# A hybrid decoder layer on one core: convolution work spread out, page numbers and embedding loaded ahead, padded rows, and norm statistics by block transposes

## The chip, the cores and the metric

The kernel runs on one core of one Trainium2 chip. The metric is the time of one execution in microseconds (us); the lower, the better. The core has a matrix engine (TensorE, PE in the profile; PEld is its loading of weights), VectorE (DVE), ScalarE (ACT), GpSimd (POOL) and SyncE (SP), which here issues nearly all transfers between device memory and the on-chip buffer SBUF. Each engine takes its instructions in the order in which they were written. An instruction that has to wait holds everything behind it on its engine.

## The reference

One layer for a prompt of 2048 tokens and for 8 sequences of 4 new tokens each with 8192 cached ones, all in fp32:

```
z = rms_norm(x) @ w_in                      # q, k, v (512 each), a, gt
u = a * sigmoid(gt)
# differential attention, 4 heads: two softmax maps (ALiBi), w = p0 - lam * p1
y_attn = rms_norm(w @ v) * (1 - lam_init)
c = causal_depthwise_conv(u, width 31) + b_dw
y_conv = silu(layer_norm(c))                # 512 channels
m = concat(y_attn, y_conv) @ w_out
h = x + rms_norm(m)
f = square(relu(rms_norm(h) @ w_ff1)) @ w_ff2          # 1024 -> 4096 -> 1024
h = h + rms_norm(f)
h = h + sigmoid(h @ w_ple_gate) * (p @ w_ple)          # p: a 256-wide embedding per token
```

For the sampled tokens keys and values come from a paged cache, whose pages a table of integers names. The outputs are h for all tokens, the keys and values, and the last 30 rows of u.

## The kernel before

Tokens lie along the free axis and channels along the 128 partitions. Every large product keeps fp32 accuracy by splitting each operand into a high and a low part: `mm3` (L234 to L236) issues hi·hi, lo·hi and hi·lo, three matmuls for each 128-deep slice. `WStream` loads the weights on SyncE (L112), makes the high part on ScalarE (L121, `wide` or `wh`) and the low part on VectorE (L122, `wlo` or `wl`), a block ahead of use. A block is 24 matmuls, eight slices of one 128-row output tile.

Three stages follow one another.

*Input projection* (to about 522 us): 80 blocks of 128x512 matmuls (`zp`) over four column blocks of the prompt. Beside them, in the background queue `bgq`, VectorE does the causal convolution of the edge columns, one filter tap of one channel tile at a time (`taps`, L246; 31 taps for each of four tiles). At the second block of the last round the kernel empties that queue at once (`while bgq: bg(1)`), then puts the layer norm over channels (`convln`) for the first 416 tokens into the queue `slow`.

*Attention* (to about 1018 us): scores `scp`, transposes, products with V; besides it runs the decode stream, `decode`, for the cached tokens (until late in the third stage). It reads the page numbers from SBUF into registers on SyncE (`feed`). At its start it loads the first row of page numbers (L921), and VectorE packs two of them into one integer (L927). GpSimd issues the 32 stores of the normed attention output (`ya`, L1130).

*Dense part* (to the end): five groups of 416 tokens (`TG`). Steps of a group g: E (output projection, 8 blocks), F1 and F2 (the two MLP products, in four chunks c of 8 blocks each, two blocks of the next F1 ahead of each F2), L (embedding product, 2 half blocks) and G (gate, 8 blocks). After each block `tick` advances every generator in the list `side` by its own rate: `norm_a` and `norm_f` (the norms around the MLP), `load_y` (the next group's input from device memory) and `convln` of the next group, whose rate is `CONV[0]` and which with `gated` also does the convolution itself, two taps to a step. `settle()` runs the whole list to its end on the spot. It is called at F1 block (3, 7) of the groups 0 to 2, after which `load_y` starts, and ahead of each E. `embed` at F2 block (3, 2) loads two tiles of p (`x`, from `pT`) and at once writes their split on ScalarE (L1647) and GpSimd.

A norm's statistic in the dense part goes over the partitions: squares are added elementwise into `acc` (128x416); `Rstd.mean` multiplies `acc`, in four pieces as the stationary operand, with a column of ones (`pm`, L149; each is two records in the profile), so that the sums lie as 128x4; `seed` finds the inverse root by three Newton steps on VectorE; `spread` (L189, `rsb`) lays the result out over all partitions by four transposes on TensorE. `convln` and the second norm of `norm_a` then copy it to SBUF on ScalarE (L312, L1545).

SBUF tiles of moving rows (`bh`, `bl`, `ah`, `al`, and views of `kv`) are 416 floats wide, 1664 bytes.

Of the kernel before, what the change touches and what calls it, by code (L numbers as in the profile page):

```python
# [20 lines left out]
NB = 8  # L21
# [9 lines left out]
TG = 416  # L31
NG = 5
# [15 lines left out]
CONV = (1.45, -2.0)  # L48
# [143 lines left out]

@with_exitstack
def kernel(
# [29 lines left out]
    odec = cp.tile([128, NH, NDEC], F32, name="odec")  # L224
    ident = cc[:, C_ID:C_ID + 128]
# [11 lines left out]

    def taps(c, u, o, n, j):

        for tap in range(NTAP):  # L240
            w = col(V_DW + j * NTAP + tap)
            x = u[:, o + tap:o + tap + n]
            if tap == 0:
                V.tensor_scalar(out=c, in0=x, scalar1=w, scalar2=col(V_BDW + j), op0=ALU.mult, op1=ALU.add)
            else:
                V.scalar_tensor_tensor(out=c, in0=x, scalar=w, in1=c, op0=ALU.mult, op1=ALU.add)  # L246
            yield

    def convln(pool, bank, n0, n, tags, gated=False):
# [55 lines left out]
        r = Rstd(nc, pool, bank, ident, n)  # L305
        r.mean(acc, ones_c[:, 0:1])
        r.seed(V)
        yield
        yield
        rsb = r.spread()  # L310
        rs = cfull[:, 4, :n]
        S.activation(out=rs, in_=rsb, func=AF.Copy)  # L312
# [70 lines left out]
    with tc.manual_schedule():  # L383
# [9 lines left out]
        with (  # L393
# [155 lines left out]
            load_x(1, 6)  # L549

# [134 lines left out]

            stores = []
# [100 lines left out]
            def lambdas():  # L787
                lt = p1.tile([128, 512], F32, tag="th", name="lt", bufs=1)[:, :256]
# [23 lines left out]
            for si, (ps, it, bl) in enumerate(steps):  # L812
# [46 lines left out]
                if ps == 0:  # L859
                    if ii == 1:  # L860
                        lambdas()
                        nc.sync.dma_start(out=udec[:, :, :, 0:30], in_=st)
                    if ii in (2, 6):
                        xtile(2 + (ii == 6))
                        for k in (0, 2, 4, 6):
                            load_x(2 + (ii == 6), k)
                    if ii in (3, 7):
                        slow.append(sumsq(2 + (ii == 7)))
                    if ii == 10:
                        bgq.append(conv_dec())  # L870
                    if ii == len(items) - 1:
                        tick(100)
                        slow.append(conversion(3))
                elif ii == 1:
                    while bgq:
                        bg(1)
                    conv_stores()
                    slow.append(convln(p1, st_bank, 0, TG, P1_TAGS))
                elif ii == 10:
                    nc.sync.dma_start(out=shared, in_=tabP)  # L880
                    load_k(0, 0)
                    for n in range(3):
                        load_q(n)
# [34 lines left out]
        def load_ids(b):  # L918
            if b < NB:
                ids[b] = dc.tile([1, NPG], I32, tag="ids", name="ids")  # L920
                nc.sync.dma_start(out=ids[b], in_=pt[:, b * NPG:b * NPG + NPG])  # L921

        def pack_ids(b):
            if b < NB:
                n = ids[b][:, :].rearrange("o (n t) -> o t n", t=2)
                ids[b] = dc.tile([1, NPG // 2], I32, tag="id2", name="id2", bufs=2)
                V.scalar_tensor_tensor(out=ids[b], in0=n[:, 1, :], scalar=1024.0, in1=n[:, 0, :], op0=ALU.mult, op1=ALU.add)  # L927
# [257 lines left out]
        with tc.tile_pool(name="p2", bufs=1, reuse_waits="tile") as p2, tc.tile_pool(name="p2ps", bufs=1, space=PSUM, reuse_waits="tile") as pp:  # L1185
# [64 lines left out]
            def combine(r):  # L1250
# [4 lines left out]
                cf = p2.tile([128, 2], F32, tag="cf", name="cf", bufs=2)  # L1255
# [75 lines left out]
            for tag, w, bufs in (("m", 8, 3), ("lp", 8, 3), ("l", 8, 4), ("cf", 2, 2)):  # L1331
# [82 lines left out]
        with (  # L1414
# [22 lines left out]

            def pair():
                return small("bh", 10, F32R), small("bl", 10, F32R)
# [11 lines left out]
            def rstd(st_, wait=1):  # L1451
                r = Rstd(nc, p3, st_bank, ident, TG)
                r.mean(st_["acc"], ones_d)
                r.seed(V)
                for _ in range(wait):
                    yield
                st_["rs"] = r.spread()
# [3 lines left out]
            def in_ring():  # L1461
# [3 lines left out]
                for i in range(RING):  # L1465
                    t = ring[:, 4 * i:4 * i + 4, :].rearrange("p a b -> p (a b)")[:, :4 * TG]
                    out.append(t.rearrange("p (l k t) -> p l k t", l=2, k=2))
                return out

            def load_y(g):  # L1470
                if g + 1 < NG:
                    yh = p3.tile([128, 8, TG], F32R, tag="ah", name="yh")
                    yl = p3.tile([128, 8, TG], F32R, tag="al", name="yl")
# [24 lines left out]
            def norm_a(g, fast):  # L1498
# [5 lines left out]
                def load(k):  # L1504
                    xs_[k] = small("bh", 10) if fast else small("x", 2)
# [6 lines left out]
                xh = p3.tile([128, 8, TG], F32R, tag="ah", name="xh")  # L1512
                xl = p3.tile([128, 8, TG], F32R, tag="al", name="xl")
# [24 lines left out]
                yield from rstd(nxt)  # L1538
                st_["rs2"] = small("rs")
                S.activation(out=st_["rs2"], in_=nxt["rs"][:, :TG], func=AF.Copy)  # L1540
# [100 lines left out]
            def embed(g):  # L1641
                h2s[g, "p"] = []
                for k in range(2):
                    p_ = small("x", 2)
                    nc.sync.dma_start(out=p_, in_=pT[:, k, g * TG:g * TG + TG])
                    ah, al = pair()
# [61 lines left out]

            def settle():
# [6 lines left out]
            pair()  # L1716
            small("acc", 2)
            small("rs")
            p3.tile([128, 8, TG], F32R, tag="al", name="yl")
            big(0)  # L1720
            big(1)
            for i in ("sq", "r", "x"):
                small(i, 2)
            for _ in load_y(0):
# [3 lines left out]
            for s_ in steps:  # L1728
                kind, g = s_[0], s_[1]
                first = s_[2:] in ((0,), (0, 0))  # L1730
                if kind == "F1" and first:
# [8 lines left out]
                    if g + 1 < NG:  # L1740
# [4 lines left out]
                            convln(p3, st_bank, (g + 1) * TG, TG, tags, not last), 1.0 if last else CONV[0], -4.0 if last else CONV[1],  # L1745
# [145 lines left out]
```

## Time and profile before

| | |
|---|---|
| time, median of 3 runs | 3175.6 us (3173.62 to 3176.58) |
| the profiled execution | 3175.43 us |
| its span, first to last instruction | 3173.6 us |
| mean granted clock of TensorE | 0.984 |
| TensorE matmul records | 18992 |
| transfers | 649.44 MB, 205 GB/s on average |

The page and the views of the trace come from that one profiled execution. A line such as `PE mm L234 <- ACT wide L121` reads: a TensorE instruction of line 234 that writes `mm` stood idle until ScalarE's instruction of line 121 had written `wide`. In timelines a row gives start, length, engine, line, operation, output and inputs with shapes, and in brackets the idle time ahead with what ended it. Line numbers are those of the kernel before.

### The profile page before, as it was taken

The numbers are of one execution on the slowest core, as the hardware profiler recorded it, in microseconds if no ns is written. First come the engines' busy times: TensorE is split into PE (matmuls) and PEld (weight loads), VectorE is DVE, ScalarE is ACT, GpSimd is POOL, SyncE is SP. The second block draws the span as 40 slices with busy tenths as digits, with TensorE's granted clock in tenths as the row PEclk, the third lists the DMA queues.
The fourth block names the chain that finished last, engine by engine and source line by source line (L and its number), as shares of the span: only waits on it lengthen the run. The fifth ranks groups of instructions, "written<-read, shape, count | busy, mean of one in ns | idle before, by whom it ended". The sixth has DMA issues, their size and how long they took to land.

```text
span 3173.6 us, 54936 instructions
## 1 busy us (share of the span) xinstructions
PE 3046.8 (96%) x18992; PEld 2680.0 (84%) x18992; DVE 2039.8 (64%) x3601; ACT 1240.9 (39%) x2248; POOL 978.6 (31%) x1063
## 2 busy tenths in 40 slices
PE   8999897999999899989999989999989999999999
PEld 6877686867778688878888878888889999999998
DVE  7889663887885677645768536767557453664444
ACT  4333223776775322224322235322244333432233
POOL 2552213766774310122301124200134121320023
PEclk9999898999999999999999989999999999999999
DMA  5445367988897876786976777877544344433334
GB/s 179 131 131 111 105 174 218 306 263 272 275 290 256 292 258 224 239 286 207 310 246 223 247 276 240 303 235 237 188 167 150 121 141 162 127 109 119 114 118 135
DMA packets 316520, 649.44 MB, mean 205 GB/s; under 512 B 45872, under 2 KB 98864, under 8 KB 315984
## 3 DMA queue, kind: packets, MB, share of 16 engines
q1 hardware_dynamic: 313680, 637.53, 62.4%
q0 software_dynamic: 2560, 8.39, 0.7%
q8 instruction: 150, 2.46, 0.3%
q14 instruction: 130, 1.06, 0.1%
HBM read 581.60 MB, written 64.18 MB: 203 GB/s over the span
## 4 chain that ended last, share of the span: by engine, by line
PE 80%; DVE 7%; DMA 3%; ACT 3%; issue 2%; POOL 2%; SPq 1%; POOLq 0%; DVEq 0%; ACTq 0%
PE mm L234 19%; PE mm L235 18%; PE mm L236 18%; PE zp L234 4%; PE zp L235 4%; PE zp L236 4%; PE dacc L1067 3%; PE ds L994 3%; PE scp L1219 3%; PE tp L1283 1%; DVE acd L653 1%; DVE wlo L122 1%; ACT S L1241 1%; DMA x<-pT 1%; PE pm L149 1%
## 5 line engine op out<-in xcount | busy, mean ns | idle before, releaser
L122 DVE TENSOR_TENSOR wlo<-wide 128x1024 fp32r<-128x1024 f32 x410 | 523.6, 1278 | 668.3 <-PE mm L235 236.1
L234 PE MATMUL mm<-bh,wide 128*128 128x416 f32 x1616 | 582.9, 361 | 25.0 <-ACT wide L121 23.9
L121 ACT ACTIVATE wide<-wide 128x1024 fp32r<-128x1024 f32 x410 | 430.8, 1053 | 411.0 <-DMA wide<-ff 252.5
L235 PE MATMUL mm<-bh,wlo 128*128 128x416 f32 x1616 | 573.7, 355 | 6.9 <-DVE wlo L122 6.8
L236 PE MATMUL mm<-bl,wide 128*128 128x416 f32 x1616 | 574.3, 355 | 0.0
L358 POOL TENSOR_TENSOR r<-r 128x416 f32<-128x416 f32 x160 | 156.4, 979 | 1067.2 <-ACT bh L1577 1067.1
L234 PE MATMUL mm<-xh,wide 128*128 128x416 f32 x1280 | 455.8, 356 | 0.0
L236 PE MATMUL mm<-xl,wide 128*128 128x416 f32 x1280 | 450.9, 352 | 0.9 <-DVE xl L1530 0.9
L235 PE MATMUL mm<-xh,wlo 128*128 128x416 f32 x1280 | 448.5, 350 | 1.5 <-DVE wlo L122 1.5
L234 PEld LDWEIGHTS mm<-bh,wide 128*128 128x128 f32 x1616 | 307.4, 190 | 56.2 <-ACT wide L121 29.1
L235 PEld LDWEIGHTS mm<-bh,wlo 128*128 128x128 f32 x1616 | 308.3, 191 | 15.6 <-DVE wlo L122 11.0
L236 PEld LDWEIGHTS mm<-bl,wide 128*128 128x128 f32 x1616 | 307.4, 190 | 4.6
L1577 ACT ACTIVATE bh<-r 128x416 fp32r<-128x416 f32 x160 | 88.2, 552 | 484.0 <-DVE r L1576 484.0
L246 DVE SCALAR_TENSOR_TENSOR ct<-ct,vc 128x416 f32<-128x416 f32 x360 | 270.6, 752 | 8.4
L234 PE MATMUL zp<-xh,wh 128*128 128x512 f32 x640 | 258.9, 404 | 10.0 <-ACT wh L121 8.5
L234 PEld LDWEIGHTS mm<-xh,wide 128*128 128x128 f32 x1280 | 240.6, 188 | 28.2 <-issue 19.6
L235 PE MATMUL zp<-xh,wl 128*128 128x512 f32 x640 | 253.3, 396 | 8.1 <-DVE wl L122 8.1
L236 PE MATMUL zp<-xl,wh 128*128 128x512 f32 x640 | 253.6, 396 | 3.6 <-DVE xl L530 3.6
L235 PEld LDWEIGHTS mm<-xh,wlo 128*128 128x128 f32 x1280 | 241.1, 188 | 5.5 <-DVE wlo L122 2.4
L236 PEld LDWEIGHTS mm<-xl,wide 128*128 128x128 f32 x1280 | 240.5, 188 | 3.6 <-DVE xl L1530 1.2
L1241 ACT ACTIVATE S<-S,m 128x512 f32<-128x512 f32 (+3 forms) x320 | 207.0, 649 | 47.3 <-DVE m L1224 46.3
L246 DVE SCALAR_TENSOR_TENSOR cv<-u,vc,cv 128x416 f32<-128x416 f32 (+1 forms) x240 | 202.9, 845 | 6.9
(249 smaller groups left out, 5119.9 us busy)
## 6 DMA issues: line engine op xcount, KB each, us to landing
wide<-ff SPq DMA_DIRECT2D x320, 512.0 KB, 4.2
kv<-ck SPq DMA_DIRECT2D x512, 256.0 KB, 4.3
kv<-cv SPq DMA_DIRECT2D x512, 256.0 KB, 4.0
wr<-w_in SPq DMA_DIRECT2D x40, 512.0 KB, 4.0
wide<-w_out SPq DMA_DIRECT2D x40, 512.0 KB, 3.3
wide<-gate SPq DMA_DIRECT2D x40, 512.0 KB, 3.8
wide<-qs SPq DMA_DIRECT2D x64, 256.0 KB, 6.3
ya<-ct SPq DMA_DIRECT2D x40, 208.0 KB, 2.1
```

The costliest lines, as they stand in the source:

```text
L121: self.nc.scalar.activation(out=hi, in_=r, func=AF.Copy)
L122: self.lo_eng(self.ns).tensor_tensor(out=lo, in0=r, in1=hi.bitcast(F32), op=ALU.subtract)
L234: T.matmul(out, wh, xh, start=start, stop=False)
L235: T.matmul(out, wl, xh, start=False, stop=False)
L236: T.matmul(out, wh, xl, start=False, stop=stop)
L246: V.scalar_tensor_tensor(out=c, in0=x, scalar=w, in1=c, op0=ALU.mult, op1=ALU.add)
L358: P.tensor_tensor(out=out, in0=a, in1=b, op=ALU.mult)
L994: T.matmul(ps[32 * k:32 * k + 32, o:o + 128 * n], qz[:, b % 2, h, :], ring[:, g:g + 4 * n, h * 128 + 32 * k:h * 128 + 32 * k + 32], start= ...
L1067: T.matmul(acc[32 * s:32 * s + 32, :], wts[u // 2 * 2][:, u % 2, 32 * s:32 * s + 32], t[i][:, s, :], start=(u == 0), stop=(s > 0 and u == ...
L1219: T.matmul(ps[:, :wp], q[:, c, l, r % 2 * 128:r % 2 * 128 + 128], kt[:, n0 % 1024:n0 % 1024 + wp], start=(l == 0), stop=(l == 1),)
L1241: S.activation(out=st_[c][:, o:e], in_=st_[c][:, o:e], func=AF.Exp, scale=-1.0, bias=st_["m"][:, c, last:last + 1], accum_out=st_["lp"][:, ...
L1577: S.activation(out=ah, in_=r, func=AF.Square)
```

## The change

Seven edits, all on order, layout and the dense part's norms; the arithmetic of matmuls stays.

1. In the projection the background queue isn't emptied at the second block: `after_conv` lets `convln` start only when the convolutions have left the queue at their usual pace, four taps a block.
2. The first row of page numbers is loaded behind the first tiles of x and packed in `lambdas` into `idp0`, a tile that lives through the kernel; `load_ids` and `pack_ids` skip row 0.
3. In the dense part `settle()` at F1 (3, 7) is gone; `behind` starts `load_y` when the entry ahead of it in `side` has ended. `CONV[0]` rises from 1.45 to 1.62.
4. `embed` is split: `load_p` at F2 (3, 0), `embed` at F2 (3, 3); for the last group at G 0 and G 3 (before G 2).
5. The 15 norms of the MLP and the four gated `convln` use `Turned`: VectorE transposes `acc` in 32x32 blocks, sums over each block's 32 columns to 128x13, one product with the block matrix `C_G` adds over partitions, Newton as before, and VectorE's block transpose of the broadcast result lays it out. ScalarE's copies go.
6. Moving rows get a pitch of `TP` = 448 floats, 1792 bytes; tile `cf` grows from 2 to 24 floats.
7. The scratch for GpSimd's transfer descriptors is 8192 bytes instead of 16384.

```diff
+TP = 448
-CONV = (1.45, -2.0)
+CONV = (1.62, -2.0)
+class Turned:
+    def gather(self, acc, turned):
+        V = self.nc.vector
+        self.part = self.small("rsp", 1)
+        V.transpose(turned, acc)
+        V.tensor_reduce(out=self.part, in_=turned.rearrange("p (b f) -> p b f", f=32), axis=AX.X, op=ALU.add)
+    def mean(self):
+        self.pm = self.bank("pm")
+        self.nc.tensor.matmul(self.pm[:, :self.nb], self.same, self.part, start=True, stop=True)
+    def seed(self, scale):
...
+    def spread(self, out):
+        self.nc.vector.transpose(
+            out.rearrange("p (b f) -> p b f", f=32),
+            self.y.rearrange("p (b o) -> p b o", o=1).to_broadcast([128, self.nb, 32]),
+        )
+        return out
...
+    idp0 = cp.tile([1, NPG // 2], I32, name="idp0")
...
+        if turned:
+            r = Turned(nc, pool, bank, cc[:, C_G:C_G + 128], n)
+            r.gather(acc, tl("sq"))
+            yield
+            yield
+            r.mean()
+            r.seed(1.0 / 512)
+            yield
+            r.spread(rs)
...
+            ids0 = p1.tile([1, NPG], I32, name="ids0")
+            nc.sync.dma_start(out=ids0, in_=pt[:, 0:NPG])
...
+            def after_conv(it, convs):
+                while any(c in bgq for c in convs):
+                    yield
+                while cstores:
+                    conv_stores()
+                yield from it
...
-                    while bgq:
-                        bg(1)
-                    conv_stores()
-                    slow.append(convln(p1, st_bank, 0, TG, P1_TAGS))
+                    slow.append(after_conv(convln(p1, st_bank, 0, TG, P1_TAGS), list(bgq)))
...
+            def moving(tag, dt=F32R):
+                return p3.tile([128, TP], dt, tag=tag, name=tag, bufs=10)[:, :TG]
...
+            def eight(tag, name):
+                return p3.tile([128, 8, TP], F32R, tag=tag, name=name)[:, :, :TG]
...
-            def rstd(st_, wait=1):
-                r = Rstd(nc, p3, st_bank, ident, TG)
-                r.mean(st_["acc"], ones_d)
-                r.seed(V)
-                for _ in range(wait):
-                    yield
-                st_["rs"] = r.spread()
+            def rstd(st_, out=None):
+                r = Turned(nc, p3, st_bank, cc[:, C_G:C_G + 128], TG)
+                r.gather(st_["acc"], small("sq", 2))
+                yield
+                r.mean()
+                r.seed(1.0 / 1024)
+                st_["rs"] = r.spread(st_bank("rsb")[:, :TG] if out is None else out[:, :])
...
+            def behind(e, it):
+                while e in side:
+                    yield
+                yield from it
...
                 if kind == "F1" and s_[2:] == (3, 7):
                     evacuate(0)
                     if g + 2 < NG:
-                        settle()
-                        side.append([load_y(g + 1), 1.0, 0.0])
-                if kind == "F2" and s_[2:] == (3, 2) and g != NG - 2:
+                        side.append([behind(side[-1] if side else None, load_y(g + 1)), 1.0, 0.0])
+                if kind == "F2" and s_[2:] == (3, 0) and g != NG - 2:
+                    load_p(min(g, NG - 2))
+                if kind == "F2" and s_[2:] == (3, 3) and g != NG - 2:
                     embed(min(g, NG - 2))
-                if s_ == ("G", NG - 2, 2):
+                if s_ == ("G", NG - 2, 0):
+                    load_p(NG - 1)
+                if s_ == ("G", NG - 2, 3):
                     embed(NG - 1)
...
-    nc = _bacc.Bacc("TRN2", target_bir_lowering=False, num_devices=1)
+    nc = _bacc.Bacc("TRN2", target_bir_lowering=False, num_devices=1, dynamic_dma_scratch_size=8192)
```

Where instructions move is seen in the order on an engine. VectorE in the input projection, at the second block of the last round, before: `cv` is the convolution, `wl` the weights' low part, `u` the convolution's input, `cmean` the channel mean that TensorE makes.

```order
L122 TENSOR_TENSOR wl<-wr,wh 128x1024
L653 SCALAR_TENSOR_TENSOR acd<-udec,vc,acd 128x32 x19
L244 TENSOR_SCALAR cv<-u,vc 128x384
L246 SCALAR_TENSOR_TENSOR cv<-u,vc,cv 128x384 x30
L122 TENSOR_TENSOR wl<-wr,wh 128x1024 x3
L775 SCALAR_TENSOR_TENSOR u<-th,fa 128x512
L293 TENSOR_TENSOR ct<-ct,cmean 128x416 x4
```

The same place in the changed kernel:

```order
L123 TENSOR_TENSOR wl<-wr,wh 128x1024
L717 SCALAR_TENSOR_TENSOR acd<-udec,vc,acd 128x32 x19
L297 TENSOR_SCALAR cv<-u,vc 128x384
L299 SCALAR_TENSOR_TENSOR cv<-u,vc,cv 128x384 x3
L123 TENSOR_TENSOR wl<-wr,wh 128x1024
L299 SCALAR_TENSOR_TENSOR cv<-u,vc,cv 128x384 x8
L123 TENSOR_TENSOR wl<-wr,wh 128x1024
L299 SCALAR_TENSOR_TENSOR cv<-u,vc,cv 128x384 x4
```

The 30 taps in one piece are now pieces of 3 to 8 between weight splits, and the mean's subtraction comes later.

ScalarE in the dense part where group 0 calls `settle`, before: L319 and L327 are the last steps of `convln`, `bh<-r` evacuates F1, `bh<-x` is `embed`.

```order
L319 ACTIVATE sq<-ct,hlb 128x416
L121 ACTIVATE wide<-wide 128x1024
L1577 ACTIVATE bh<-r 128x416 x2
L319 ACTIVATE sq<-ct,hlb 128x416
L327 ACTIVATE ct<-ct 128x416
L319 ACTIVATE sq<-ct,hlb 128x416
L327 ACTIVATE ct<-ct 128x416
L319 ACTIVATE sq<-ct,hlb 128x416
L327 ACTIVATE ct<-ct 128x416 x2
L121 ACTIVATE wide<-wide 128x1024 x2
```

The same steps in the changed kernel, where they begin earlier:

```order
L381 ACTIVATE sq<-ct,hlb 128x416 x2
L1156 ACTIVATE sc<-dacc 128x512
L122 ACTIVATE wide<-wide 128x1024
L389 ACTIVATE ct<-ct 128x416
L122 ACTIVATE wide<-wide 128x1024
L1654 ACTIVATE bh<-r 128x416
L381 ACTIVATE sq<-ct,hlb 128x416
L389 ACTIVATE ct<-ct 128x416
L122 ACTIVATE wide<-wide 128x1024
```

Seven of the norm's steps stood between two weight splits; now one or two do.

VectorE at the start of attention, before: L1224 takes a row of scores with its maximum, L1256 to L1258 are softmax's sums, L927 packs page numbers.

```order
L1224 ISA m 128x1
L1256 TENSOR_REDUCE l<-lp 128x2
L1257 RECIPROCAL cf<-l 128x1
L1258 SCALAR_TENSOR_TENSOR cf<-l,nlam,cf 128x1
L927 SCALAR_TENSOR_TENSOR id_4369<-ids 1x32
L1256 TENSOR_REDUCE l<-lp 128x2
L1257 RECIPROCAL cf<-l 128x1
L1258 SCALAR_TENSOR_TENSOR cf<-l,nlam,cf 128x1
L1224 ISA S_4388,m<-scp,shared 128x512
```

In the changed kernel:

```order
L1330 SCALAR_TENSOR_TENSOR cf<-l,nlam,cf 128x1
L1328 TENSOR_REDUCE l<-lp 128x2
L1329 RECIPROCAL cf<-l 128x1
L1330 SCALAR_TENSOR_TENSOR cf<-l,nlam,cf 128x1
L1296 ISA S_4330,m<-scp,shared 128x384
L1296 ISA m 128x1
L1296 ISA S_4337,m<-scp,shared 128x384
L1296 ISA m 128x1
L1296 ISA S_4342,m<-scp,shared 128x512
```

The row L927 is gone there (its like stands in the projection), so a row of scores follows the sums of the row before it directly.

More of the change, by code (lines that the diff above doesn't have):

```diff
@@ L190, in spread, with __init__, small @@
         return r[:, :self.n]
+class Turned:
+    def __init__(self, nc, pool, bank, same, n):
+        self.nc, self.pool, self.bank, self.same, self.n, self.nb = nc, pool, bank, same, n, n // 32
+    def small(self, tag, bufs=2):
+        return self.pool.tile([128, 16], F32, tag=tag, name=tag, bufs=bufs)[:, :self.nb]
+    def gather(self, acc, turned):
[7 more added lines that the diff above has]
+    def seed(self, scale):
+        V = self.nc.vector
+        x, y, t = self.small("rsx", 1), self.small("rsy"), self.small("rst", 1)
+        V.tensor_scalar(out=x, in0=self.pm[:, :self.nb], scalar1=scale, scalar2=EPS, op0=ALU.mult, op1=ALU.add)
+        V.tensor_scalar(
+            out=y.bitcast(I32), in0=x.bitcast(I32), scalar1=-0.5, scalar2=1597463007.0, op0=ALU.mult, op1=ALU.add
+        )
+        for _ in range(3):
+            V.tensor_tensor(out=t, in0=y, in1=x, op=ALU.mult)
+            V.scalar_tensor_tensor(out=t, in0=t, scalar=-0.5, in1=y, op0=ALU.mult, op1=ALU.mult)
+            V.scalar_tensor_tensor(out=y, in0=t, scalar=1.5, in1=y, op0=ALU.add, op1=ALU.mult)
+        self.y = y
+    def spread(self, out):
+        self.nc.vector.transpose(
+            out.rearrange("p (b f) -> p b f", f=32),
+            self.y.rearrange("p (b o) -> p b o", o=1).to_broadcast([128, self.nb, 32]),
+        )
+        return out
 @with_exitstack
@@ L236, in mm3, with pack @@
         T.matmul(out, wh, xl, start=False, stop=stop)
+    def pack(out, ids):
+        n = ids[:, :].rearrange("o (n t) -> o t n", t=2)
+        V.scalar_tensor_tensor(out=out, in0=n[:, 1, :], scalar=1024.0, in1=n[:, 0, :], op0=ALU.mult, op1=ALU.add)
     def taps(c, u, o, n, j):
@@ L304, in convln @@
         yield
-        r = Rstd(nc, pool, bank, ident, n)
-        r.mean(acc, ones_c[:, 0:1])
-        r.seed(V)
-        yield
-        yield
-        rsb = r.spread()
-        rs = cfull[:, 4, :n]
-        S.activation(out=rs, in_=rsb, func=AF.Copy)
+        rs = cfull[:, 4, :n]
+        if turned:
[7 more added lines that the diff above has]
+            r.spread(rs)
+        else:
+            r = Rstd(nc, pool, bank, ident, n)
+            r.mean(acc, ones_c[:, 0:1])
+            r.seed(V)
+            yield
+            yield
+            S.activation(out=rs, in_=r.spread(), func=AF.Copy)
         yield
@@ L923, in pack_ids @@
         def pack_ids(b):
[L924 to L925 removed]
+            if 0 < b < NB:
+                raw = ids[b]
                 ids[b] = dc.tile([1, NPG // 2], I32, tag="id2", name="id2", bufs=2)
[L927 removed]
+                pack(ids[b], raw)
+        ids[0] = idp0
         def decode():
@@ L1511, in norm_a @@
                 yield from rstd(st_)
-                xh = p3.tile([128, 8, TG], F32R, tag="ah", name="xh")
-                xl = p3.tile([128, 8, TG], F32R, tag="al", name="xl")
+                xh, xl = eight("ah", "xh"), eight("al", "xl")
                 xs2[g] = [(xh[:, k, :], xl[:, k, :]) for k in range(8)]
@@ L1537, in norm_a @@
                     yield
-                yield from rstd(nxt)
-                st_["rs2"] = small("rs")
-                S.activation(out=st_["rs2"], in_=nxt["rs"][:, :TG], func=AF.Copy)
+                rs2 = small("rs")
+                yield from rstd(nxt, rs2)
+                st_["rs2"] = rs2
                 yield
@@ L1645, in embed @@
                     nc.sync.dma_start(out=p_, in_=pT[:, k, g * TG:g * TG + TG])
+                    h2s[g, "x"].append(p_)
+            def embed(g):
+                h2s[g, "p"] = []
+                for p_ in h2s[g, "x"]:
                     ah, al = pair()
@@ L1716 @@
             pair()
+            eight("al", "yl")
             small("acc", 2)
-            small("rs")
-            p3.tile([128, 8, TG], F32R, tag="al", name="yl")
             big(0)
@@ L1723 @@
                 small(i, 2)
+            eight("ah", "yh")
             for _ in load_y(0):
```

30 lines of the change are left out of this document (15 added, 15 removed).

## Prediction

> **What bounds the kernel now.** I read the page's totals first, then the list of what TensorE waits for, then busy times stretch by stretch around its longest stops.
>
> ```profile
> span 3173.6 us, 54936 instructions
> PE 3046.8 (96%) x18992; PEld 2680.0 (84%) x18992; DVE 2039.8 (64%) x3601; ACT 1240.9 (39%) x2248; POOL 978.6 (31%) x1063
> ```
>
> TensorE works 3046.8 of 3173.6 us. The profiled execution took 3175.4 us (its span and 1.8 around it), 0.2 under the median of the runs, 3175.6; I sum against 3175.4 and read the result as a median. About 127 us are not TensorE work, so a change can win only these, or make TensorE's own work shorter. The waits, as total, times, longest:
>
> ```profile
> PE mm L234 <- ACT wide L121: 23.9, 6, 7.0
> PE mm L235 <- DVE wlo L122: 10.4, 16, 1.0
> PE cmean L290 <- POOL shared L355: 5.8, 1, 5.8
> ```
>
> Few and long waits: the places matter, not the averages. The next view gives such places, with three undisturbed stretches for comparison. Its columns: stretch, length, busy time (and count) of PE, PEld, DVE, ACT and POOL, TensorE's granted clock (PEclk), DMA share, GB/s.
>
> ```profile
> 325.00:360.00 35.00, 21.55 (x74) 16.40 (x73) 16.63 (x25) 4.43 (x7) 5.38 (x4) 0.76 0.49 157
> 515.00:560.00 45.00, 28.94 (x130) 22.16 (x128) 22.68 (x84) 21.04 (x59) 19.18 (x30) 0.81 0.86 240
> 600.00:1000.00 400.00, 379.74 (x3666) 299.48 (x3665) 320.29 (x922) 278.98 (x735) 281.76 (x391) 1.00 0.87 273
> 1100.00:1370.00 270.00, 269.07 (x1728) 236.47 (x1727) 186.02 (x283) 74.83 (x101) 39.69 (x41) 1.00 0.72 241
> 1250.00:1300.00 50.00, 50.00 (x286) 42.72 (x286) 42.56 (x58) 13.53 (x17) 11.19 (x10) 1.00 0.80 270
> 1370.00:1390.00 20.00, 14.23 (x61) 13.27 (x60) 9.55 (x11) 6.47 (x10) 6.92 (x7) 0.83 0.64 207
> 1395.00:1410.00 15.00, 11.51 (x68) 9.94 (x70) 4.79 (x6) 5.48 (x8) 6.27 (x5) 0.89 0.84 296
> 1840.00:1860.00 20.00, 14.49 (x80) 12.30 (x80) 10.32 (x13) 6.46 (x10) 7.23 (x8) 0.74 0.58 200
> 1868.00:1885.00 17.00, 12.53 (x75) 10.54 (x74) 6.01 (x8) 5.54 (x9) 6.26 (x5) 0.80 0.81 295
> 2305.00:2340.00 35.00, 26.55 (x126) 24.97 (x125) 17.73 (x29) 13.26 (x21) 13.12 (x13) 0.85 0.57 199
> 3050.00:3115.00 65.00, 62.46 (x330) 60.10 (x329) 37.69 (x51) 29.71 (x47) 27.43 (x22) 1.00 0.35 113
> ```
>
> Length less PE busy is idle time. A stop also costs clock: the granted clock falls to half two to five us into a long stop and stays there for 3.4 to 10.2 us. I count that loss as (1 − PEclk) × length, less half of the idle time that lies inside the half-clock part (found by narrowing the stretches: 7.6 us of idle in 325–360, 8.2 in 515–560, 1.0 in 1370–1390, 3.3 in 1840–1860, 1.6 in 1868–1885, 4.8 in 2305–2340). Undisturbed, 1100 to 1370 us, TensorE is idle 0.93 of 270 us while VectorE is busy 69%.
>
> **The change, part by part.** *Input projection.*
>
> ```profile
> 314.21 21.58 DVE L246 SCALAR_TENSOR_TENSOR cv<-u,vc,cv 128x384 f32<-128x384 f32 x30
> ```
>
> VectorE's timeline shows 30 filter taps done in one go, 21.6 us, and TensorE stops at 329 us for the weight split (`wl`) queued behind them. A second stop is the channel mean behind GpSimd's sums (5.8, above). 325–360: idle 13.45, clock 0.24 × 35 = 8.4 less half of 7.6 idle = 4.6. Now the taps come four to a block and the norm starts behind them; the same work lies beside matmuls. **−18.1.** If the pace left a stop, it would be one split's delay, counted in the leftovers.
>
> *Page numbers.* At the start of attention VectorE's queue, in order, holds the packing of page numbers:
>
> ```profile
> 539.56 0.18 DVE L927 SCALAR_TENSOR_TENSOR id<-ids 1x32 int32<-1x32 int32 x1 [10.54 <-DMA ids<-pt]
> ```
> ```profile
> wide<-qs SPq DMA_DIRECT2D x6, 256.0 KB, 9.2
> ```
>
> VectorE stands 10.54 us for a load (`ids<-pt`) that the load queue has behind V and K parts. Loaded in the projection, it is gone; its 0.18 us of packing stays, elsewhere. 515–560 holds 16.1 idle and 0.19 × 45 = 8.6 less half of 8.2 = 4.5 clock: 20.5. Not all returns: the attention's own query tiles of the same queue take 9.2 us to land (second row's median, in 515–560), and the next are issued just behind. Bounds −4 and −15; I take **−10**.
>
> *Settle.* Before, three of the five groups force the convolution's norm to its end at the last FF1 block. ScalarE's timeline there:
>
> ```profile
> 1371.09 0.64 ACT L319 ACTIVATE sq<-ct,hlb 128x416 f32<-128x416 f32 x1 [2.31 <-DVE ct L317]
> ...
> 1377.81 1.99 ACT L121 ACTIVATE wide<-wide 128x1024 fp32r<-128x1024 f32 x2
> ```
>
> For 6.7 us ScalarE follows VectorE through the norm's last steps, and two weight splits stand behind them: the 23.9 us row of waits. Now the norm ends by its own pace, a weight split between any two of its steps, and its eight stores lie between weight loads. Idle 5.77 + 5.51 + 7.5 (of 8.45; 0.9 is the embedding's) = 18.8; clock 0.17 × 20 less 0.5, 0.26 × 20 less 1.7, 0.15 × 35 less 2.4 = 9.0. **−27.8.** Next in time is the load of the next group's input, `yh`, which is now let go by the norm's end and needed only with the next output projection, after eight FF2 blocks of some 4.5 us (24 matmuls, 0.19 apart): the same place as before.
>
> *Embedding.* ScalarE's in-order queue holds the split of a tile whose load was issued just then:
>
> ```profile
> 1398.86 1.10 ACT L1647 ACTIVATE bh<-x 128x416 fp32r<-128x416 f32 x2 [6.65 <-DMA x<-pT]
> ```
>
> Issued three blocks of 4.5 us ahead, 13 us against the 6.65 waited, the load lands before its split. 1395–1410: 3.49 + 0.11 × 15 = 5.1. 1868–1885: 4.47 + 0.20 × 17 less 0.8 = 7.1. With 0.9 in the third group and, near the end of the program, 2.5 of 65 in the last stretch: **−15.6.**
>
> *Norms.* On TensorE one norm in the dense part reads:
>
> ```profile
> 2398.59 0.35 PE L236 MATMUL mm<-bl,wide 128*128 128x416 f32 x1
> 2398.78 0.95 PE L149 MATMUL pm<-ones_d,acc 128*128 128x1 f32 x8
> 2399.59 0.44 PE L234 MATMUL mm<-bh,wide 128*128 128x416 f32 x1
> 2399.86 0.35 PE L235 MATMUL mm<-bh,wlo 128*128 128x416 f32 x1
> ...
> 2404.22 0.60 PE L189 MATMUL rsb<-cc,rsy 128*128 128x128 f32 x4
> 2404.58 0.43 PE L234 MATMUL mm<-bh,wide 128*128 128x416 f32 x1
> ```
>
> Matmuls start 0.19 apart. The eight column records take 0.81 and the matmul behind them 0.27 instead of 0.19: 0.89. The four transposes take 0.36 and, I take it, the same 0.08: 0.44. Both go; one 128x13 product comes, between nothing and 0.44; by its two records of 0.1 and the 0.08 I take 0.2. 19 × (0.89 + 0.44 − 0.2) = **−21.5.** In exchange VectorE gets, per norm, two block transposes and a reduction:
>
> ```profile
> L1048 DVE STREAM_TRANSPOSE wt<-sc 128x256 f32<-128x256 f32 x64 | 27.5, 434 | 0.0
> L562 DVE TENSOR_REDUCE accd<-xnd 128x32 f32<-128x256 f32 x1 | 0.6, 622 | 0.0
> L246 DVE SCALAR_TENSOR_TENSOR ct<-ct,vc 128x416 f32<-128x416 f32 x360 | 270.6, 752 | 8.4
> ```
>
> By elements 2 × 0.71 + 1.01 = 2.4 us, 46 us over 19. Behind them queue the low halves of the weights (`wlo`). The convolution's pace also rises from 2.9 to 3.24 taps a block at 752 ns, at most 0.26 us more per block; its sum stays. Price for TensorE between 0 (row 1100–1370) and 46 (all of it). All `wlo` waits today are 10.4 us in 16 stops; I let them double: **+10.**
>
> *Padded rows.* Dense matmuls stream 416-column rows of 1664 bytes, 6.5 times 256, so every other one starts 128 bytes off a multiple of 256.
>
> ```profile
> 2692.64 0.35 PE L234 MATMUL mm<-kp,wide 128*128 128x416 f32 x1
> 2693.21 0.35 PE L234 MATMUL mm<-kp,wide 128*128 128x416 f32 x1
> 2693.78 0.35 PE L234 MATMUL mm<-kp,wide 128*128 128x416 f32 x1
> 2694.34 0.35 PE L234 MATMUL mm<-kp,wide 128*128 128x416 f32 x1
> ```
>
> Triples start 0.57 or 0.56 apart. Over the undisturbed ones of all 3280 the mean is 562 ns for rows on a multiple and 571 for the others. After the change rows are 1792 bytes, 7 × 256, and all have the same start; by the layout all of them, and the weights too, move to 128 past a multiple. If what counts is the row's distance to the weights, all are like today's fast half: 1640 × 9 ns = −15 (−21 if the alternation costs too). If the row's start itself counts, all are slow: +15. The trace doesn't separate them; I take the distance, since one common shift of both operands otherwise would have to matter: **−15.**
>
> The Trainium skill ("TensorE: Matmul & The Clock Gate", Part 2: What happens when you issue a matmul) says that loading weights doesn't steal SBUF read bandwidth from the running matmul, since each has a read port. By it the distance to the weights couldn't matter, and all rows would be slow, +15, a sum of 3113; this trace shows the alternation, but moves weights and rows never separately, so no row here decides.
>
> *Leftovers.* Each new product may find its sums late (`pm` waited once for `acc` before, 1.8 us), and one restart may keep part of a stop. **+6.** ScalarE's copies and the stores' new places cost nothing: ScalarE is 39% busy. The halved descriptor scratch: nothing, see the last rival.
>
> Sum: −18.1 − 10 − 27.8 − 15.6 − 21.5 + 10 − 15 + 6 = −92.0; 3175.4 − 92.0 = 3083.4, say **3083**.
>
> **Rivals.** *(a) The row's start counts.* All rows slow: 3083 + 30 = 3113. For it: only the start is known to differ between today's halves. Against: weights move as well.
> *(b) VectorE becomes the bound in the dense part.* Where the convolution is densest, 1250–1300, it is already busy 42.56 of 50. Faster taps and transposes there would hold `wlo`; if all 46 us show, 3083 + 36 = 3119. Against: 85% leaves room for 7 us per 50, and the additions are some 3.
> *(c) The attention's start does not do what is meant:* TensorE, freed at 529, stops a few us later at the next query tile, gain 0: 3093.
> *(d) Slower.* GpSimd issues attention's output stores, through descriptors in the scratch that is halved:
>
> ```profile
> q0 software_dynamic: 2560, 8.39, 0.7%
> ```
> ```profile
> DMA to landing us min/median/max: 1.9/5.4/7.8
> ```
>
> ```profile
> L1130 POOL DMA_DIRECT2D ya<-yh x16: 587/587/724, 578.8 to 1036.0; - x16
> ```
>
> 32 stores, in 16 pairs, of 80 packets each. If the descriptors of two consecutive ones no longer fit, GpSimd waits for the landing of the one before, 31 × 5.4 = 167 us, on an engine busy 282 of 400 us at 600–1000 whose scaled scores TensorE transposes: 3083 + 167 = 3250. It makes the kernel slower once more than 92 us of it show, 17 full waits. Against: the pairs lie some 30 us apart (16 from 578.8 to 1036.0), and each store has landed within 8.
>
> The Trainium skill ("SBUF — State Buffer", SBUF size: 192, 224, or 256?) gives 16 KiB per partition for this scratch; what half of it holds no run here shows.
>
> **How the numbers follow.** Forecast 0.50, (a) 0.25, (b) 0.10, (c) 0.08, (d) 0.04, and 0.03 that the stops return elsewhere and the time stays within 0.2% of before, which is about what a measurement of this kernel can tell from no change. Low end: full attention gain (−5), alternation (−6), no price on VectorE (−10) come near 3063. High end: (a) with part of (b), 3121. So 3063 to 3121 leaves out (d), the worst of (b), and what I have overlooked. Faster 0.93, same 0.03, slower 0.04.
>
> **What would show it.** PEclk 1.00 and PE busy near the length in the stretches above, around 330, 1370, 1400, 1845, 1870, 2310; if not, the step of that stretch is wrong. The row `mm L234 <- ACT wide` under 3 us. One `pm` row per norm about 0.2 long, no `rsb` matmul after 1018 us. `wlo` waits near 20 us; 40 or more is (b). Starts of `mm` triples even, 562 ns or less; 571 is (a). GpSimd's `ya` stores about 0.6 us each; several us is (d). The forecast fails most easily by the rows, the one term for which only a choice stands.

## The result, and the profile after

The changed kernel takes 3098.3 us, the median of four runs (3097.4 to 3101.9); the kernel before took 3176.1 in the runs beside it (3173.6 to 3179.3). The ratio is 0.9757, with a 95% interval of 0.974 to 0.9774. The forecast was 3083, the range 3063 to 3121: faster, as forecast, by 78 us where 92 were expected. The lines of the page that answer to those of before:

```profile
span 3096.8 us, 54549 instructions
PE 3006.8 (97%) x18802; PEld 2649.6 (86%) x18802; DVE 2083.5 (67%) x3658; ACT 1236.1 (40%) x2239; POOL 992.7 (32%) x1063
```

What TensorE waits for in the changed kernel (total, times, longest):

```profile
PE mm L283 <- DVE wlo L123: 13.7, 14, 3.3
PE scp L1291 <- DVE m L1296: 8.4, 13, 1.8
...
PE scp L1291 <- DMA wide<-qs: 6.1, 3, 2.7
PE dacc L1139 <- DMA kv<-cv: 5.4, 1, 5.4
...
PE mm L282 <- DMA yh<-ya: 3.3, 1, 3.3
PE pm L216 <- DVE rsp L212: 2.6, 1, 2.6
...
PE mm L282 <- ACT wide L122: 1.7, 5, 0.4
```

The 23.9 us behind ScalarE's weight splits have become 1.7, and the 11.6 us stop behind `m` is gone. New is the load of `yh`, and query tiles cost 6.1 us where they cost 0.9 before. The busy times of the changed kernel by stretch (columns as before: stretch, length, PE, PEld, DVE, ACT, POOL, PEclk, DMA share, GB/s):

```profile
325.00:360.00 35.00, 35.00 (x156) 28.96 (x155) 21.46 (x30) 9.13 (x13) 4.41 (x4) 1.00 0.45 145
500.00:545.00 45.00, 35.10 (x192) 25.70 (x192) 30.79 (x110) 28.60 (x83) 25.87 (x35) 0.89 0.91 252
1075.00:1345.00 270.00, 268.36 (x1712) 236.52 (x1713) 202.52 (x302) 80.47 (x110) 45.95 (x48) 1.00 0.73 248
1340.00:1375.00 35.00, 35.00 (x251) 31.29 (x250) 15.01 (x22) 11.47 (x17) 8.70 (x9) 1.00 1.00 362
1830.00:1860.00 30.00, 30.00 (x204) 27.48 (x202) 11.32 (x15) 10.31 (x14) 4.32 (x4) 1.00 0.94 323
2240.00:2290.00 50.00, 50.00 (x270) 49.77 (x269) 25.27 (x40) 18.97 (x29) 11.70 (x11) 1.00 0.63 201
2655.00:2740.00 85.00, 78.09 (x401) 75.16 (x400) 69.24 (x113) 33.63 (x53) 36.09 (x29) 0.98 0.36 114
```

In the projection (first row) and where groups 0, 1 and 2 used to stop (fourth to sixth row) TensorE is busy all the time at full clock. The second row, the start of attention, is better but not clean. The last row shows a loss that is new: 6.9 us idle with VectorE busy 81% (before, 2710 to 2810 us hold only 2.4 us of idle time).

The same by stages, worked out from the records of both traces: idle is the time between TensorE's records; clock is half of TensorE's busy time in half-clock parts; work is the rest. Attention ends here where the first output projection starts, at 994 us before (not at the 1018 us named above), and the dense part with the last matmul, 5.8 and 5.9 us ahead of the span's end.

| stage | before: length = idle + clock + work | after | change |
|---|---|---|---|
| projection | 522.8 = 34.7 + 8.0 + 480.1 | 505.2 = 19.9 + 5.0 + 480.4 | −17.6 |
| attention | 471.5 = 36.2 + 6.1 + 429.1 | 475.4 = 34.8 + 10.5 + 430.2 | +3.9 |
| dense part | 2173.5 = 50.0 + 20.5 + 2103.1 | 2110.3 = 29.5 + 10.6 + 2070.2 | −63.2 |

So the gain comes from the projection and the dense part as foreseen, and attention, where 10 us were expected, gave none; 3.3 us of its new length are the wait for `yh`. The projection's gain has no run of its own, but it stands in every trace: 503.7 to 505.2 us in the ten with that edit, 522.1 to 524.2 in the four without.

### The profile page after: what moved, and what is told of

It reads as the page before. It is cut to its first block, busy times and chain, and to the rows that moved or that the text cites. A ratio compares the mean times of both kernels' runs of the same rounds, so it can differ in the third digit from the quotient of the medians.

```text
span 3096.8 us, 54549 instructions
## 1 busy us (share of the span) xinstructions
PE 3006.8 (97%) x18802; PEld 2649.6 (86%) x18802; DVE 2083.5 (67%) x3658; ACT 1236.1 (40%) x2239; POOL 992.7 (32%) x1063
## 4 chain that ended last, share of the span: by engine, by line
PE 83%; DVE 5%; DMA 5%; issue 2%; ACT 2%; POOL 1%; SPq 1%; POOLq 0%; DVEq 0%; ACTq 0%
PE mm L282 19%; PE mm L283 19%; PE mm L284 19%; PE zp L282 4%; PE dacc L1139 4%; PE zp L284 4%; PE zp L283 4%; PE ds L1066 3%; PE scp L1291 3%; PE tp L1355 1%; DMA kv<-ck 1%; DMA wide<-qs 1%; DMA vs<-fh 1%; DVE wlo L123 1%; PE ov L282 1%
## 5 line engine op out<-in xcount | busy, mean ns | idle before, releaser
L123 DVE TENSOR_TENSOR wlo<-wide 128x1024 fp32r<-128x1024 f32 x410 | 529.8, 1292 | 591.4 <-issue 204.2
L282 PE MATMUL mm<-bh,wide 128*128 128x416 f32 x1616 | 574.1, 355 | 1.5 <-ACT sq L1527 1.2
L283 PE MATMUL mm<-bh,wlo 128*128 128x416 f32 x1616 | 567.3, 351 | 7.9 <-DVE wlo L123 7.9
L284 PE MATMUL mm<-bl,wide 128*128 128x416 f32 x1616 | 566.4, 350 | 0.0
L299 DVE SCALAR_TENSOR_TENSOR cv<-u,vc,cv 128x416 f32<-128x416 f32 (+1 forms) x240 | 209.3, 872 | 6.7
```

Of the source, the lines that this page charges most:

```text
L123: self.lo_eng(self.ns).tensor_tensor(out=lo, in0=r, in1=hi.bitcast(F32), op=ALU.subtract)
L282: T.matmul(out, wh, xh, start=start, stop=False)
L283: T.matmul(out, wl, xh, start=False, stop=False)
L284: T.matmul(out, wh, xl, start=False, stop=stop)
```

## The experiments

Each was run beside the kernel before. "Undo" means the changed kernel with one part taken back.

**Rows alone.** Two kernels tell what about a row's place counts: before plus padded rows on multiples of 256 bytes like the weights, and the same with the rows shifted by 128. Both also have the halved scratch, and tiles in another order.

```diff
+TP = 448
+                return p3.tile([128, TP], dt, tag=tag, name=tag, bufs=10)[:, :TG]
...
+            p3.tile([128, 32], F32, name="shift")
```

The last line is in the second kernel alone, which shifts its views of `kv` likewise.

> The kernel before with padded rows alone: every moving row of the dense part starts on a multiple of 256 bytes, as the weights do (and the halved descriptor scratch, which makes room). Theory (the distance of row and weights counts): all matmuls run like the fast half of before, start to start 188.0 ns on average instead of 189.4, so 9840 x 1.4 ns = 14 us less, about 3162. Rival (the pitch counts, rows must not alternate, wherever they lie): the same 3162. Rival (rows have no effect of their own): 3176.

> As x6_rows, with all moving rows shifted by 128 bytes while the weights stay: every row is 128 off a multiple of 256 and 128 off its weights. Theory (distance to the weights): all matmuls run like the slow half of before, 190.7 ns, 13 us above before, about 3189, some 27 above x6_rows. Rival (the row's start itself): the same 3189, but then the changed kernel, whose rows also start at 128, could not show 188.0 ns. Rival (pitch): no difference to x6_rows, 3162.

Measured: 3168.7 (ratio 0.9979, 0.997 to 0.9989) and 3173.6 (0.9993, 0.9983 to 1.0002). On average matmuls start 188.1 ns apart in the first and 188.2 in the second, against 188.0 and 190.7 in the two halves of before, 189.4 on average. So rows that alternate cost time, as the rival said, and rows of one pitch are no slower on average when they lie 128 off their weights. But the second average hides two kinds of blocks. Its hi·hi matmuls, every third one, early and late in the dense part:

```profile
1099.74 0.35 PE L235 MATMUL mm<-xh,wide 128*128 128x416 f32 x1
...
1104.22 0.35 PE L235 MATMUL mm<-xh,wide 128*128 128x416 f32 x1
```
```profile
2800.02 0.35 PE L235 MATMUL mm<-xh,wide 128*128 128x416 f32 x1
...
2804.58 0.35 PE L235 MATMUL mm<-xh,wide 128*128 128x416 f32 x1
```

The eight triples between them take 560 ns each in the first, 570 in the second. Whole blocks run at the one or the other: the mean is 187.2 ns a matmul up to 2200 us and 189.6 from 2400 to 3000 (`x6_rows`: 187.9 and 188.3). So rows 128 off their weights can run nearly as slowly as the slow half of before, and what switches the blocks is not shown.

In the dense part the work falls by 10.8 and 9.4 us. Less than that reaches the end, in the second kernel so little that its time can't be told from before. In both, as in the changed kernel, the load of `yh` is late (below), 2.2 and 2.4 us; the rest of the difference lies in idle time and clock.

**Page numbers alone**, on the kernel before:

```diff
+            ids0 = p1.tile([1, NPG], I32, name="ids0")
+            nc.sync.dma_start(out=ids0, in_=pt[:, 0:NPG])
...
+                pack(idp0, ids0)
```

> The kernel before with the page numbers' edit alone; its small tile shifts weights and rows by 128 bytes together, half the rows at distance 0 as before. Theory: the 11.6 us wait on VectorE at the start of attention goes, but TensorE then waits 2 to 5 us for query tiles, so it is some 6 us ahead an eighth into attention; transfers and clock take most of it back, 1 to 4 us are left at the first output projection: 3172 to 3175. Rival (as forecast): 10 us stay, 3166. Rows by distance: those that start at 128 run at 188 ns, those on a multiple of 256 at 190.7, the opposite of before.

Measured: 3175.1 (1.0002, 0.9992 to 1.0012), no gain. The waits of TensorE in attention, first before, then with the edit:

```profile
PE scp L1219 <- DVE m L1224: 21.1, 13, 11.6
PE ov L234 <- ACT o L1305: 4.6, 5, 2.1
...
PE scp L1219 <- DMA wide<-qs: 0.9, 1, 0.9
```
```profile
PE scp L1230 <- DVE m L1235: 11.7, 17, 2.2
PE ov L235 <- ACT o L1316: 7.9, 5, 3.5
PE scp L1230 <- DMA wide<-qs: 4.7, 2, 2.8
...
PE ds L1005 <- DMA kv<-ck: 2.0, 1, 2.0
```

The long stop goes (21.1 to 11.7), and 8 of those 9 us return on query tiles, pages and the eviction of outputs. In the profiled execution, 6 us slower than the median, TensorE is 10 us ahead at 541 us, 4.5 at 656, and 3 behind at 788, after 6.8 us of half clock from 781 on. The rows behave as expected: by the layout, those that start where the weights start (now 128) take 188.0 ns, the others 190.7, the reverse of before.

**The load of `yh`.** In the changed kernel the first output projection waits for its input. SyncE's timeline, and the matmul that waits:

```profile
955.67 0.35 SPq L984 DMA_DIRECT2D kv<-cv  x1
975.72 0.39 SPq L1558 DMA_DIRECT2D yh<-ya  x1
```
```profile
980.62 0.71 PE L282 MATMUL mm<-yh,wide 128*128 128x416 f32 x1 [3.25 <-DMA yh<-ya]
```

SyncE stands 20 us before that load. By the layout, wider tiles and another order of allocation had put `yh` on the probability tiles (`wth`) that attention's last products read, so the load had to wait for them.

```diff
-            for i in ("sq", "r", "x"):
-                small(i, 2)
-            eight("ah", "yh")
+            eight("ah", "yh")
+            for i in ("sq", "r", "x"):
+                small(i, 2)
```

> The changed kernel with the tile of the first output projection's input placed ahead of three small tiles, so that it no longer lies on tiles that attention's last products read. Theory: its load starts as soon as before the change, the 3.3 us wait and 3.4 us of half clock behind it at 977 us go: 5 to 7 us less, 3092 to 3093. Rival (the load is late because of the page loads ahead in the same queue): no gain, 3098.

Measured: 3097.0 (0.9738 to 0.977), a miss: the tile now lay on the last score tiles, which are read nearly as late, and the load issued at 977 us again. Placed between `r` and `x`, it lies on tiles that are free early, as before the change:

```diff
-            for i in ("sq", "r", "x"):
+            for i in ("sq", "r"):
                 small(i, 2)
             eight("ah", "yh")
+            small("x", 2)
```

> The changed kernel with the input tile of the first output projection (yh) on the same attention tiles as before the change: a score tile and two key tiles that are free some 200 instructions before attention ends, not on the last probability tiles (changed kernel) or the last score tiles (x1_yh). Theory: its load issues some 15 us earlier, before GpSimd's last stores, the 3.3 us wait at the first output projection and the 3.4 to 5 us of half clock behind it go: 3098 - 7 = 3091. Rival (late for the transfers ahead of it): no change, 3098.

Measured: 3092.5 (ratio 0.9733, 0.972 to 0.9747). The load issues at once, and no matmul waits for it:

```profile
961.40 0.39 SPq L1558 DMA_DIRECT2D yh<-ya  x1
```

The changed kernel thus paid some 6 us for where a tile had been put; the intervals of the two kernels overlap a little.

**The old norm statistics back in the dense part**, otherwise the changed kernel:

```diff
-                r = Turned(nc, p3, st_bank, cc[:, C_G:C_G + 128], TG)
-                r.gather(st_["acc"], small("sq", 2))
+                r = Rstd(nc, p3, st_bank, ident, TG)
+                r.mean(st_["acc"], ones_d)
...
```

The rest of the edit gives the gated `convln` its old statistic and the copies on ScalarE.

> The changed kernel with the old norm statistics in the dense part (eight column records and four transposes on TensorE, copies on ScalarE) at the places of the new. Theory: TensorE gets back 19 x 1.1 = 21 us, VectorE's waits fall by 3 to 7 us: 3098 + 14 to 18 = 3112 to 3116. Rival (VectorE's added work costs TensorE what the prediction says, 10, or more): 3109 or less; were all 46 us to show, the kernel would be faster than the changed one.

Measured: 3102.5 (0.976 to 0.9787), 4 above the changed kernel (0.974 to 0.9774), so the times alone hardly part the two; the traces do. Against the changed kernel, TensorE's work in the dense part rises by 17.1 us, and idle and clock fall by 13.9, 11.9 of them in the last two groups. Both sides of the exchange are there, and nearly cancel. A likely reason is seen where the changed kernel waits longest for `wlo`, in TensorE's timeline, then VectorE's:

```profile
2668.38 0.45 PE L283 MATMUL mm<-bh,wlo 128*128 128x416 f32 x1 [3.26 <-DVE wlo L123]
```
```profile
2665.05 0.17 DVE L228 SCALAR_TENSOR_TENSOR rsy<-rst,rsy 128x13 f32<-128x13 f32 x1
2665.26 0.63 DVE L233 STREAM_TRANSPOSE rsb<-rsy 128x416 f32<-128x416 f32 x1
2665.92 0.65 DVE L1595 SCALAR_TENSOR_TENSOR big<-big,vc,rsb 128x416 f32<-128x416 f32 x1
2666.60 0.59 DVE L1598 TENSOR_TENSOR big<-big,x 128x416 f32<-128x416 f32 x1
2667.11 1.22 DVE L123 TENSOR_TENSOR wlo<-wide 128x1024 fp32r<-128x1024 f32 x1
```

Newton's steps, the transpose and the first use of its result stand in one piece ahead of the weight split; the old statistic had a step's pause (a `yield`) between Newton and the transposes. No run puts such a pause into the new one, so whether the missing pause or VectorE's added work makes the stop stays open.

**The forced norm back**, with its former pace:

```diff
-CONV = (1.62, -2.0)
+CONV = (1.45, -2.0)
...
-                        side.append([behind(side[-1] if side else None, load_y(g + 1)), 1.0, 0.0])
+                        settle()
+                        side.append([load_y(g + 1), 1.0, 0.0])
```

> The changed kernel with the convolution's norm forced to its end at the last FF1 block again, and its former pace. Theory: three stops of 5 to 7 us of idle and 2.7 to 3.5 us of clock each come back, 28 us: 3126. Rival (the new norms shorten the forced chain, so less comes back): 3112 to 3120, with stops of 3 to 4 us at the same places.

Measured: 3132.8 (0.9846 to 0.9876), 34 above the changed kernel. The row of waits is back,

```profile
PE mm L282 <- ACT wide L122: 23.6, 8, 8.5
```

with stops of 6.2, 6.2 and 8.5 us where before they were 4.7, 4.7 and 7.0: with the new statistic the stops are longer, not shorter; no run shows why.

**The embedding in one place again:**

```diff
-                if kind == "F2" and s_[2:] == (3, 0) and g != NG - 2:
+                if kind == "F2" and s_[2:] == (3, 2) and g != NG - 2:
                     load_p(min(g, NG - 2))
-                if kind == "F2" and s_[2:] == (3, 3) and g != NG - 2:
                     embed(min(g, NG - 2))
...
```

The lines left out do the same for the last group, at G 2.

> The changed kernel with the embedding's load and split in one place again, at FF2 block (3, 2). Theory: stops of 2.6 to 3.8 us idle, with 1.7 to 2.6 us of clock in two groups, come back: 3098 + 16 = 3114. Rival (ScalarE waited only since its queue was disturbed by the forced norm just ahead): 3098 to 3103.

Measured: 3113.5 (0.9773 to 0.9808; four runs lie at 3109 to 3115, one at 3100), 15 above by the medians. The waits for weight splits, 1.7 and 13.7 us in the changed kernel, grow:

```profile
PE mm L283 <- DVE wlo L123: 19.4, 18, 3.3
PE mm L282 <- ACT wide L122: 7.9, 7, 2.5
```

In the dense part idle and clock rise by 16.6 us in all. So the embedding's stop doesn't need the forced norm ahead of it.

**Attention's start, two more.** First the 1 MB table of the decode scores later, then the page numbers' edit undone, both on `x9_yh2`:

```diff
-            nc.sync.dma_start(out=tab, in_=tabD)
             yield 0.0
...
             yield 0.0
+            nc.sync.dma_start(out=tab, in_=tabD)
```

> x9_yh2 with the 1 MB table of the decode scores (tab) loaded some 60 transfers later, behind the query tiles that attention waits for. Theory (what the page numbers' edit won at the start of attention is lost to transfers in front of TensorE's data): the waits on query tiles at the start, 2.1 and 2.7 us, and half clock behind them go, 3092 - 5 to 8 = 3085 to 3088. Rival (attention as a whole is paced by the sum of its transfers): the waits turn up on the page loads (ds) instead, 3090 to 3094.

```diff
-            if 0 < b < NB:
+            if b < NB:
...
-                pack(idp0, ids0)
```

> x9_yh2 without the page numbers' edit: they are loaded and packed at the start of attention again. Theory: the 11 us wait on VectorE is back, but the stops on query tiles and pages after it go, and the time is that of x9_yh2 within 3: 3090 to 3096. Rival (the forecast's value of the edit): 3092 + 10 = 3102.

Measured: 3092.7 (0.9722 to 0.9764) and 3095.1 (0.9731 to 0.9758), against 3092.5. The table isn't what holds the query tiles: with it out of the way they cost 5.0 us in four waits. And without the edit the stop is there,

```profile
PE scp L1287 <- DVE m L1292: 22.7, 16, 11.2
```

but the time is only 2.7 us longer (3.5 by the ratios, as the two ran on different chips): of attention, 38.6 us are idle and 8.4 lost to the clock, against 32.2 and 13.0 with the edit.

**The best of both norms.** On `x9_yh2`, the new statistic in groups 0 to 2 and in the convolution, the old one in the last two groups; beside it `x9_yh2` once more (`x9_again`):

```diff
+                if old:
+                    r = Rstd(nc, p3, st_bank, ident, TG)
...
+                yield from rstd(st_, old=g >= NG - 2)
```

> x9_yh2 with the old norm statistics in the last two groups alone (TensorE's column products and transposes), the new in the first three and in the convolution. Theory (the new norms cost TensorE more on VectorE's weight splits than they save, where they wait in the last two groups, and less in the first three): idle and clock lost from 2280 us to the end fall by some 9, TensorE's own work rises by some 3: 3092 - 6 = 3086. Rival (the idle in the last groups has another cause, such as the gate's loads): 3092 to 3096.

> x9_yh2 once more, on the same chip as x12_hybrid, so that the two can be compared: 3092 as before, within 3.

Measured on one chip: 3088.5 (0.9706 to 0.9734) and 3092.3 (0.972 to 0.9746). From 2260 us on the waits for `wlo` are 11.5 us in 11 stops in the changed kernel, 11.1 in 11 in `x9_again` and, with the old statistic there,

```profile
PE mm L283 <- DVE wlo L123: 3.0, 5, 1.0
```

Against `x9_again`, idle and clock in the last two groups fall by 7.4, the work rises by 4.6. The median is the lowest of all, 10 us below the changed kernel's and 4 below that of `x9_again`, though these last two intervals overlap.

## Why the prediction was right, and where it was wrong

*Input projection, −18.1.* Right: −17.6 in the two traces.

*Page numbers, −10 (bounds −4 to −15).* This is the step that failed: it is worth 0.7 us on the kernel before and about 3 on the changed one, and rival (c) was right here. The stop did go. What the step missed is that TensorE came to other waits, for query tiles, pages and ScalarE's evictions, and that short stops in attention also cost clock. That the new waits are the old transfers arriving at their former time is argued from them, and moving the one large transfer didn't shorten them; which transfers set the pace stays open.

*Settle and embedding, −27.8 and −15.6.* Right together: from 1080 us (1086 in the changed kernel) to the end of group 2 idle and clock fell from 48.3 to 6.3 us. That is −42.0 against −40.9, the two terms without the 2.5 near the program's end, where idle time fell by 1.4. Undone one at a time they cost 34 and 15. (The clock part of the first, as its factors stand, is 9.2 and not 9.0, a rounding.)

*Norms, −21.5 on TensorE and +10 for VectorE.* The mechanism was right, the exchange worse: −17.1 and +13.9, a gain of 3 where 11.5 were forecast. One product costs what was taken, so where 4 us of TensorE's saving went is open. Its surroundings in the changed kernel:

```profile
2330.55 0.35 PE L284 MATMUL mm<-bl,wide 128*128 128x416 f32 x1
2330.73 0.29 PE L216 MATMUL pm<-rsp,cc 128*128 128x13 f32 x2
2330.87 0.44 PE L282 MATMUL mm<-bh,wide 128*128 128x416 f32 x1
2331.15 0.35 PE L283 MATMUL mm<-bh,wlo 128*128 128x416 f32 x1
```

From the matmul ahead to the second behind it 0.60 us pass, where two plain steps take 0.38: 0.22 against the 0.2 taken. VectorE's instructions were cheaper than estimated, and still cost more than estimated:

```profile
L211 DVE STREAM_TRANSPOSE sq<-acc 128x416 f32<-128x416 f32 x19 | 11.4, 602 | 0.0
L212 DVE TENSOR_REDUCE rsp<-sq 128x13 f32<-128x416 f32 x19 | 11.2, 588 | 0.7
L233 DVE STREAM_TRANSPOSE rsb<-rsy 128x416 f32<-128x416 f32 x10 | 6.3, 627 | 0.3
```

1.8 us a norm, 34 in all instead of 46. Their sum alone doesn't set the price, since all groups have such norms and nearly all the loss is in two. Rival (b) put the danger where the convolution is densest; there almost nothing was lost (third row of stretches, 1.6 us idle of 270 at VectorE 75%, against 0.9 before). It was in the last two groups.

*Padded rows, −15.* The size was near: 1.4 ns × 9840 matmuls = 14 us by the starts (the prediction's 9 ns a triple is 3 × 2.7 = 8 by them). The reason is not borne out. The step chose the row's distance to the weights; in `x7_rows_off`, where every row is 128 off, the average is 188.2 ns, not 190.7. Yet the distance isn't out either: late blocks there run at 189.6, and with alternating rows the slow half was each time the one that starts elsewhere than the weights (190.7 ns, in before and in `x2_ids_only`). The start alone, rival (a), is out: by the layout the changed kernel's rows all start at 128, and they run at 188.0. The Trainium skill says that weight loads don't take read bandwidth from the moving stream ("TensorE: Matmul & The Clock Gate", Part 2: What happens when you issue a matmul), which the prediction weighed against the distance. The fast blocks of `x7_rows_off` agree with that, and its slow ones leave it undecided.

*Leftovers, +6.* The size was right by accident: the late load of `yh` alone is worth 6.

*The slower side (d).* The halved scratch shows nothing. GpSimd's issues of the stores, changed kernel:

```profile
L1202 POOL DMA_DIRECT2D ya<-yh x16: 587/587/722, 555.0 to 1025.8; - x16
```

587 ns in the middle, as before. The 15 us between forecast and result are then mainly attention (7 to 9 by the single edits; 14 in the two traces, of which 3.3 are the wait for `yh`, counted above with the leftovers) and the norms' exchange (7 by the times, 8 by the traces), with 1 to 4 of the rows.

## What to carry to other kernels

A removed wait is worth what the next one leaves: before counting it, look which data the engine would need a few microseconds later and when those arrive. Work moved from the busy engine to a less busy one costs by its place in that engine's queue, so keep the old form where that queue has no slack; a pause between the pieces is worth trying, though no run here has tried it. After any change of tile sizes or of the order of allocation, see on which older tiles the first tiles of the next stage now lie.

## What the runs showed of the hardware that was not expected

*A short stop can halve the clock, or not.* The same stop of attention, before and in the changed kernel, in TensorE's timeline (first of each pair) and the stretch behind it:

```profile
652.88 1.33 PE L1219 MATMUL scp<-K,wide 128*128 128x256 f32 x4 [1.78 <-DVE m L1224]
```
```profile
652.90:662.50 9.60, 9.29 (x53) 5.77 (x54) 9.12 (x35) 8.18 (x24) 5.70 (x7) 1.00 0.77 202
```
```profile
630.44 1.34 PE L1291 MATMUL scp<-K,wide 128*128 128x256 f32 x4 [1.76 <-DVE m L1296]
```
```profile
630.50:640.10 9.60, 9.50 (x48) 5.77 (x49) 8.30 (x32) 7.31 (x23) 4.77 (x6) 0.82 0.74 216
```

1.78 us cost no clock (1.00), 1.76 us cost 0.18 of 9.6 us. Within a trace the half-clock parts begin on a raster of 3.413 us: those at 632.17, 669.71 and 806.25 us lie 11 and 40 of it apart. Laid over the two stops, the raster tells them apart. The stop of the changed kernel lies almost wholly in one window of it (first row), and the clock falls at that window's end. The stop before is cut in two by a boundary at 652.20:

```profile
628.76:632.17 3.41, 1.62 (x9) 0.75 (x12) 3.34 (x12) 1.40 (x5) 2.13 (x3) 1.00 1.01 272
```
```profile
648.78:652.20 3.42, 2.32 (x16) 1.88 (x15) 1.97 (x7) 2.68 (x9) 0.00 (x0) 1.00 0.80 224
652.20:655.61 3.41, 2.63 (x15) 1.22 (x16) 3.27 (x12) 1.57 (x5) 2.12 (x3) 1.00 0.74 198
```

TensorE is busy for 48% of the first window, and for 68% and 77% of the other two. Over both traces, from 60 us to 10 us before the end, all 18 full-clock windows with TensorE busy less than 45% were followed by half clock, and only 3 of 1722 with 57% or more. So a stop of this length costs clock or not by where it falls. The Trainium skill ("TensorE: Matmul & The Clock Gate", Part 1: The HAM clock gate) has a free-running window of 3413 ns, with which that agrees, and lets the clock fall after an idle window of about 3.4 us, with which it doesn't: a window in which TensorE was busy 48% of the time was enough here. Attention lost 6 to 14 us to the clock in the 14 profiles, a spread that is about the spread of whole runs of one kernel (25 runs of before: 3170.7 to 3182.3).

*Rows of one pitch.* Averaged over the dense part, 416-column fp32 matmuls start 188.0 to 188.2 ns apart when all moving rows start alike modulo 256 bytes, and 189.4 when starts alternate. Whole blocks keep one of two paces: about 187 or 188 ns with rows and weights alike (`x6_rows`), 187 or 190 with rows 128 off (`x7_rows_off`).
